# Three weight tiles of a GEMV moved from the input projection to W_out, and half of the last shift's weights moved to the end of the stream

## The chip, the cores and the metric

The kernel runs on one core of a Trainium2 chip. The metric is the device time of that core in microseconds (us): the median of three runs is given for a kernel, and one further execution was recorded by the profiler. Everything is in fp32.

## The reference

One residual block over a sequence of 256 tokens with 2048 features, conditioned by one vector `c` (adaLN). Cut to what matters:

```
mod = silu(c) @ w_ada + b_ada                      # 6 vectors of 2048
sh1, sc1, gt1, sh2, sc2, gt2 = split(mod, 6)
h = rms_norm(x, g_mix) * (1 + sc1) + sh1
qa, ka, va, qb, kb, vb = split(h @ w_in)           # 16 heads A (4 key heads), 16 heads B
o = concat[rms_norm(attention_A), rms_norm(attention_B)]
x = x + gt1 * (o @ w_out)
h = rms_norm(x, g_ffn) * (1 + sc2) + sh2
y = moe(h)      # top-1 group of 4, then top-2 of its 8 experts; 32 gated MLPs 2048-512-2048
x = x + gt2 * y
shf, scf = split(silu(c) @ w_ada_final + b_ada_final, 2)
out = rms_norm(x, g_final) * (1 + scf) + shf
```

The weights of the 32 experts are 403 MB of the 596 MB that are read. The products of a vector with `w_ada` and `w_ada_final` (GEMVs) need 117 MB more, and each weight of them is used once.

## The kernel before

**The stream.** All large weights pass through one ring of six slots of 2 MB in SBUF (class `Ring`, lines 42 to 79). Tiles are numbered in the order in which `ring.add` is called. SP loads tile i once the program has released tiles 0 to i−6 and the engine that used the slot is through with it (`pump`, issue at L70 and L72); a later tile never overtakes an earlier one. So the slowest consumer of an early tile holds up all loads behind it.

**Stages.** The first quarters (L294 to L360) form the first adaLN vectors, transpose and modulate x into `hT`, and compute the projections for the attention of kind A. Then a list `order` (L116 to L123) of 20 tiles for PE follows: 12 of `w_in` for the heads of kind B (`in_step`, L574) and 8 of `w_out` (`out_step`, L607). W_out tiles 0 to 3 multiply the A half of `o` and 4 to 7 the B half, each for 512 of the 2048 output columns and two token halves t, 8 products for each half; after each half DVE updates x from the PSUM bank `po` (L622). The B half is scaled by `r_oB`, which `norm_o` makes out of the sum of squares over all 16 heads (L539) by a matmul with ones (L546) and six small operations on DVE (L190 to L198).

**Vector tiles.** Behind each PE tile the table `VECTOR_TILES` (L39) puts so many vector tiles in the ring: 4 x 128 rows and 1024 columns of `w_ada` or `w_ada_final`. DVE sums them into an accumulator 128 x 1024, four operations for each (`vec_step`: L382 opens the accumulator, L384 adds). Four such tiles make one half of a vector. `vec_steps` takes them from a queue and stops where a new half begins while two accumulators are in use. An accumulator comes free with `vec_finish`, three turns after its last tile; that of a half of gt1 comes free when `spread_gt1(1)` or `spread_gt1(3)` has run, at W_out tiles 1 and 3. The halves stand in the order sh2, sc2, gt2, gt1, scf (two of each), then the first half of shf.

**Weaving.** In between PE's tiles `weave` advances the attention heads, which wait on the same DVE, and due items of the list `later`.

**Routing.** `router_turns(n)` and `router_products(n)` transpose x and form the router's logits. The second half of the shift vector shf (columns 1024 to 2047) is not summed by DVE: four ring tiles of 4 x 128 rows pass through PE with `cact` (silu of c, one column per 128 rows) broadcast as the stationary operand, 8 products for each tile, 32 in all (`shift_step`, L683 to L702). Then DVE finds group and experts, PE makes prefix sums (`pp`, L749 to L753), and the MoE begins: 8 passes over 4 experts each, gate and up products L829, down products L857.

**The end.** L1057 to L1078: the two rows of PSUM that make the last shift available on all partitions, the last norm, the scaled x plus shift, and the stores from ACT and SP.

Of the kernel before, what the change touches and what calls it, by code (L numbers as in the profile page):

```python
# [23 lines left out]
D = 2048  # L24
# [11 lines left out]
NEG = -1e30  # L36
RING = 6

VECTOR_TILES = [2, 3, 2, 3, 2, 3, 2, 3, 2, 3, 2, 3, 2, 2, 2, 2, 3, 2, 1, 0]  # L39


ROW_ADA, ROW_FIN, ROW_MIX, ROW_FFN, ROW_GFIN, ROW_OA, ROW_OB = 0, 24, 32, 36, 40, 44, 46
# [42 lines left out]
def block_kernel(ctx: ExitStack, tc: tile.TileContext, a: dict):  # L85
# [22 lines left out]
        first_quarters.append((gemv, [ring.add((2, 1536), rows(w_in, q * 512 + h * 256, 2, 0, 1536)) for h in range(2)]))  # L108

    vec_tiles = []  # L110
    for name, w, col in (("sh2", ada, 3 * D), ("sc2", ada, 4 * D), ("gt2", ada, 5 * D), ("gt1", ada, 2 * D), ("scf", fin, D), ("shf", fin, 0)):
        for c in (0,) if name == "shf" else (0, 1024):
            vec_tiles += [((name, c // 512), k, 4, 1024, rows(w, k * 512, 4, col + c, 1024)) for k in range(4)]
    blocks = [("qB0", 1536), ("kB0", 2560), ("vB0", 3584), ("qB1", 2048), ("kB1", 3072), ("vB1", 4096)]
    pe_tiles = [(name, h, rows(w_in, h * 1024, 8, col, 512)) for name, col in blocks for h in range(2)]
    pe_tiles += [("wo", h * 4 + n, rows(w_out, h * 1024, 8, n * 512, 512)) for h in range(2) for n in range(4)]  # L116
# [5 lines left out]
        order.append((name, h, part, extra))  # L122
    assert not vec_tiles  # L123

    shf_tiles = [ring.add((4, 1024), rows(fin, 512 * i, 4, 1024, 1024)) for i in range(4)]


    moe_tiles = []
    for g in range(8):
        e0 = 4 * g  # L130
        gu = []
        for J in range(4):
            for w in ("w_gate", "w_up"):
# [77 lines left out]
    with ExitStack() as sa:  # L211
# [305 lines left out]
        def values(kind, h):  # L517
# [12 lines left out]
            if h % 2:  # L530
# [3 lines left out]
                if c == 0:  # L534
                    S.activation(s, op[:, 0:256], AF.Square)
                else:
                    s2 = pa2.tile([128, SEQ], F32, tag="sq", name=f"sq{kind}{c}", bufs=1)
                    S.activation(s2, op[:, 0:256], AF.Square)
                    G.tensor_tensor(s, s, s2, op=ALU.add)  # L539
                if h == 15:  # L540
                    later.append([1, lambda: norm_o(kind)])

# [428 lines left out]
    for g in range(8):  # L971
# [56 lines left out]
        else:  # L1028
# [3 lines left out]
            for fc in range(4):  # L1032
# [33 lines left out]
    diag = pb1.tile([128, 128], F32, name="diag")
    S.activation(diag, ident, AF.Identity, scale=r3[:, 1:2])
    for J, y in last.items():
        c = slice(J * 512, (J + 1) * 512)
        PE.matmul(y, lhsT=diag, rhs=big[:, 1, c], start=False, stop=True)  # L1070
        S.copy(big[:, 1, c], y)  # L1071
        S.dma_start(out=out[:, 1, c], in_=big[:, 1, c])  # L1072
    for t, J, store in ((0, 0, 0), (0, 1, 2), (0, 2, 0), (0, 3, 2), (1, 0, 1)):
        c = slice(J * 512, (J + 1) * 512)
        V.scalar_tensor_tensor(big[:, t, c], big[:, t, c], r3[:, t : t + 1], shbc[:, c], op0=ALU.mult, op1=ALU.add)
        if store:
            c = slice((J + 1 - store) * 512, (J + 1) * 512)
            nc.sync.dma_start(out=out[:, t, c], in_=big[:, t, c])  # L1078
# [26 lines left out]
```

## Time and profile before

| | before |
|---|---|
| median of 3 runs | 1508.41 us (1505.83 to 1509.24) |
| the profiled execution | 1502.64 us, its span 1501.0 us |
| PE busy, share of the span | 1188.0 us, 79% |
| DVE busy | 499.0 us, 33% |
| HBM read | 596.02 MB, mean 398 GB/s over the span |
| granted TensorE clock, mean | 0.917 |

The span runs from the first to the last instruction. Times in the trace are counted from its start. The trace records each fp32 product of the program as two instructions: the 8 products of one half of a W_out tile read as x16. A granted clock of 1.00 is the upper of TensorE's two levels, 2.4 GHz.

### The profile page before, as it was taken

What the parts mean: (1) busy time and instruction counts of PE and PEld (TensorE: products, weight loads), DVE (VectorE), ACT (ScalarE), POOL (GpSimd) and SP (SyncE); (2) the same over time, 40 slices, a digit from 0 to 9 for tenths busy, and PEclk for the clock granted to TensorE, in tenths of its full rate; (3) what the DMA queues carried; (4) which work ended last, traced back from release to release, by engine and by line L of the source; (5) the groups of instructions that cost most, each with busy time, mean ns of one, the idle gap of its engine ahead of it and who ended that gap; (6) DMA issues with size and microseconds to landing.
All of it is one profiled execution on the core that took longest, in us unless ns stands there. A gap on an engine that the chain in (4) does not pass through costs nothing.

```text
span 1501.0 us, 14175 instructions
## 1 busy us (share of the span) xinstructions
PE 1188.0 (79%) x5891; PEld 525.8 (35%) x5892; DVE 499.0 (33%) x807; ACT 166.2 (11%) x423; POOL 157.5 (10%) x144
## 2 busy tenths in 40 slices
PE   4889999999999997777677767766767667667786
PEld 2667865754444542222212212211211211221222
DVE  1453789887667531011111211111201201111113
ACT  2000222223220110000000100000000000000012
POOL 1000355523441100000000000000000000000002
PEclk9999999999999999978978889889889988997999
DMA  9999999999987999999999999999999999999995
GB/s 333 396 392 399 394 402 402 402 401 400 355 317 302 388 380 422 421 420 421 421 421 421 421 421 422 422 422 421 421 420 422 422 422 422 421 421 421 421 412 210
DMA packets 125470, 599.38 MB, mean 399 GB/s; under 512 B 5881, under 2 KB 8489, under 8 KB 78041
## 3 DMA queue, kind: packets, MB, share of 16 engines
q1 hardware_dynamic: 121248, 594.82, 98.1%
q10 hardware_dynamic: 4120, 3.57, 0.7%
q8 instruction: 48, 0.79, 0.2%
q14 instruction: 22, 0.17, 0.0%
q0 software_dynamic: 32, 0.02, 0.0%
HBM read 596.02 MB, written 2.12 MB: 398 GB/s over the span
## 4 chain that ended last, share of the span: by engine, by line
DMA 45%; PE 11%; SPq 0%; issue 0%; ACT 0%; DVE 0%; ACTq 0%; DVEq 0%
DMA ring<-w_down 23%; DMA ring<-w_up 12%; DMA ring<-w_gate 10%; PE yp L857 5%; PE gp L829 2%; PE up L829 2%; PE sc_g L876 0%; SPq L70 0%; PE bc L770 0%; PE bc L771 0%; PE last L1060 0%; PE last L1059 0%; ACT big L1071 0%; PE last L1070 0%; ACTq L1072 0%
## 5 line engine op out<-in xcount | busy, mean ns | idle before, releaser
L857 PE MATMUL yp<-ring,actT_g 128*32 128x512 f32 x1024 | 181.5, 763 | 97.5 <-DMA ring<-w_down 91.7
L829 PE MATMUL up<-ring,xg_g 128*32 128x512 f32 x1024 | 177.3, 721 | 73.3 <-DMA ring<-w_up 73.2
L829 PE MATMUL gp<-ring,xg_g 128*32 128x512 f32 x1024 | 169.9, 703 | 69.3 <-DMA ring<-w_gate 68.8
L878 DVE TENSOR_TENSOR x<-x,sc_g 128x512 f32<-128x512 f32 x64 | 44.0, 688 | 252.3 <-PE sc_g L876 252.3
L618 PE MATMUL po<-ring,oT 128*128 128x512 f32 x256 | 118.0, 617 | 1.4 <-DMA ring<-w_out 1.4
L857 PEld LDWEIGHTS yp<-ring,actT_g 128*32 128x32 f32 x1024 | 39.3, 133 | 225.6 <-DMA ring<-w_down 130.9
L881 POOL TENSOR_TENSOR big<-x,xg_gscf 128x512 f32<-128x512 f32 x8 | 10.0, 1272 | 958.8 <-DVE x L878 958.8
L799 DVE TENSOR_SCALAR xg_g<-g_g,gsc,sh2c 128x128 f32<-128x128 f32 x64 | 26.2, 410 | 249.8 <-PE g_g L790 232.5
L829 PEld LDWEIGHTS up<-ring,xg_g 128*32 128x32 f32 x1024 | 38.4, 127 | 197.5 <-DMA ring<-w_up 105.9
L829 PEld LDWEIGHTS gp<-ring,xg_g 128*32 128x32 f32 x1024 | 38.0, 123 | 186.5 <-DMA ring<-w_gate 99.5
L797 ACT ACTIVATE xg_g<-g_g,sh2c,gsc 128x128 f32<-128x128 f32 x64 | 29.3, 458 | 503.9 <-DVE xg_g L799 503.9
L384 DVE SCALAR_TENSOR_TENSOR acc_gt<-ring,cact,acc_gt 128x1024 f32<-128x1024 f32 x60 | 79.2, 1321 | 1.6
L870 DVE TENSOR_TENSOR ys_g<-yp,gt2bc 128x512 f32<-128x512 f32 x32 | 21.8, 690 | 171.8 <-PE yp L857 171.8
L618 PEld LDWEIGHTS po<-ring,oT 128*128 128x128 f32 x256 | 49.7, 198 | 63.6 <-issue 61.1
L790 PEld LDWEIGHTS g_g<-pn_g,big 128*128 128x128 f32 x512 | 60.5, 194 | 29.1 <-issue 28.2
L790 PE MATMUL g_g<-pn_g,big 128*128 128x128 f32 x512 | 66.7, 284 | 1.4 <-DVE pn_g L782 1.4
L348 PE MATMUL qA<-hT,ring 128*128 128x256 f32 x256 | 61.6, 396 | 4.8 <-DVE hT L343 3.5
L876 PE MATMUL sc_g<-ys_g,smat_g 128*128 128x512 f32 x128 | 63.4, 618 | 1.6 <-DVE ys_g L870 1.6
L585 PE MATMUL pw_vB<-ring,hT 128*128 128x512 f32 x128 | 56.7, 597 | 2.9 <-DMA ring<-w_in 2.9
L589 PE MATMUL pw_kB<-hT,ring 128*128 128x256 f32 x256 | 57.0, 381 | 1.2 <-DMA ring<-w_in 1.2
L589 PE MATMUL pw_qB<-hT,ring 128*128 128x256 f32 x256 | 56.5, 381 | 0.2 <-DMA ring<-w_in 0.2
L348 PEld LDWEIGHTS qA<-hT,ring 128*128 128x128 f32 x256 | 50.7, 199 | 13.1 <-DVE hT L343 4.3
(329 smaller groups left out, 1125.4 us busy)
## 6 DMA issues: line engine op xcount, KB each, us to landing
ring<-w_gate SPq DMA_DIRECT2D x64, 2048.0 KB, 20.3
ring<-w_up SPq DMA_DIRECT2D x64, 2048.0 KB
ring<-w_down SPq DMA_DIRECT2D x62, 2048.0 KB, 20.4
ring<-w_ada SPq DMA_DIRECT2D x32, 2048.0 KB, 17.0
ring<-w_ada SPq DMA_DIRECT2D x32, 1024.0 KB, 14.1
ring<-w_ada_final SPq DMA_DIRECT2D x16, 2048.0 KB, 11.0
ring<-w_in SPq DMA_DIRECT2D x12, 2048.0 KB, 16.8
ring<-w_out SPq DMA_DIRECT2D x8, 2048.0 KB
```

The source lines that it names most:

```text
L348: PE.matmul(early[n // 2][:, (n % 2) * 256 : (n % 2 + 1) * 256], lhsT=w[:, n * 128 : (n + 1) * 128], rhs=hT[:, kk, :], start=kk == 0 and n ...
L384: V.scalar_tensor_tensor(accs[name], w[:, kk, :], cact[:, c : c + 1], accs[name], op0=ALU.mult, op1=ALU.add)
L585: PE.matmul(b[s], lhsT=hT[:, kk, s * 128 : (s + 1) * 128], rhs=w[:, k, :], start=kk == 0, stop=kk == 15)
L589: PE.matmul(b[s][:, n * 256 : (n + 1) * 256], lhsT=w[:, k, c * 128 : (c + 1) * 128], rhs=hT[:, kk, :], start=kk == 0 and n == 0, stop=kk = ...
L618: PE.matmul(b, lhsT=oT[:, (i // 4) * 8 + k, t * 128 : (t + 1) * 128], rhs=w[:, k, :], start=k == 0, stop=k == 7)
L790: PE.matmul(pm[:, i * 128 : (i + 1) * 128], lhsT=big[:, t, kk * 128 : (kk + 1) * 128], rhs=pn[:, t, :], start=t == 0 and i == 0, stop=t == ...
L797: S.activation(xg[:, kk, :], pm[:, i * 128 : (i + 1) * 128], AF.Identity, bias=sh2c[:, kk : kk + 1], scale=gsc2[:, kk : kk + 1])
L799: V.tensor_scalar(xg[:, kk, :], pm[:, i * 128 : (i + 1) * 128], gsc2[:, kk : kk + 1], sh2c[:, kk : kk + 1], op0=ALU.mult, op1=ALU.add)
L829: PE.matmul(bankt[32 * e : 32 * e + 32, :], lhsT=xg[:, kk, 32 * e : 32 * e + 32], rhs=w[e // 2][:, e % 2, j, :], start=kk == 0, stop=kk == ...
L857: PE.matmul(y[32 * e : 32 * e + 32, :], lhsT=aT[:, fc, 32 * e : 32 * e + 32], rhs=w(e)[:, n * 512 : (n + 1) * 512], start=fc == 0, stop=fc ...
L876: PE.matmul(pm, lhsT=sm[:, t * 128 : (t + 1) * 128], rhs=ys[:, n, :], start=True, stop=True)
L878: V.tensor_tensor(x1[:, t, c], x1[:, t, c], pm, op=ALU.add)
```

## The change

Three things are changed. (1) `VECTOR_TILES` gives 27 instead of 30 vector tiles to the input projection and 17 instead of 14 to W_out, and the halves of the vectors are queued in another order: both halves of gt1 ahead of the second half of gt2. (2) The second half of shf is split into two blocks of 512 columns. The first (columns 1024 to 1535) is loaded as two tiles of 8 x 128 rows during routing, 16 products, all behind the router's last products. The second (1536 to 2047) comes as two such tiles behind the last tile of the MoE, and the last sums, copies and updates are written anew for it. (3) The sum of squares of the last head is added on DVE instead of POOL.

```
-VECTOR_TILES = [2, 3, 2, 3, 2, 3, 2, 3, 2, 3, 2, 3, 2, 2, 2, 2, 3, 2, 1, 0]
+VECTOR_TILES = [2, 2, 3, 2, 2, 2, 3, 2, 2, 3, 2, 2, 3, 2, 3, 3, 3, 2, 1, 0]
...
+    for i in (0, 1, 2, 3, 4, 6, 7, 5, 8, 9, 10):
+        name, w, col, c = halves[i]
+        vec_tiles += [((name, c // 512), k, 4, 1024, rows(w, k * 512, 4, col + c, 1024)) for k in range(4)]
...
-    shf_tiles = [ring.add((4, 1024), rows(fin, 512 * i, 4, 1024, 1024)) for i in range(4)]
+    shf_tiles = [ring.add((8, 512), rows(fin, 1024 * i, 8, 1024, 512)) for i in range(2)]
...
+    last_block = [(c0, c1, ring.add((c1 - c0, 512), rows(fin, c0 * 128, c1 - c0, 1536, 512))) for c0, c1 in ((0, 8), (8, 16))]
...
-                    G.tensor_tensor(s, s, s2, op=ALU.add)
+                    (V if h == 15 else G).tensor_tensor(s, s, s2, op=ALU.add)
...
-            for k in range(4):
-                for J in (2, 3):
-                    PE.matmul(
-                        shift[32 * J : 32 * J + 32, :], lhsT=cact[:, 4 * i + k : 4 * i + k + 1].to_broadcast([128, 32]),
-                        rhs=w[:, k, (J - 2) * 512 : (J - 1) * 512], start=i + k == 0, stop=i + k == 6, skip_group_check=True,
-                    )
+            for k in range(8):
+                q = 64 + 32 * (k % 2)
+                PE.matmul(
+                    shift[q : q + 32, :], lhsT=cact[:, 8 * i + k : 8 * i + k + 1].to_broadcast([128, 32]),
+                    rhs=w[:, k, :], start=i == 0 and k < 2, stop=i == 1 and k > 5, skip_group_check=True,
+                )
...
-        shift_step(0)
         router_turns(3)
-        shift_step(1)
         router_products(3)
-        for i in (2, 3):
+        for i in range(2):
             shift_step(i)
...
-                    spread(R["shf"], ROW_FIN, shbc)
+                    spread(R["shf"], ROW_FIN, shbc, range(2))
+                    four = pb1.tile([128, 2], F32, name="four")
+                    V.tensor_reduce(four[:, 0:1], ident[:, 0:128:32], axis=AX.X, op=ALU.add)
+                    V.tensor_reduce(four[:, 1:2], ident[:, 64:128:32], axis=AX.X, op=ALU.add)
+                    pm = mbank("m", "bc", 2)
+                    PE.matmul(pm, lhsT=four[:, 1:2].to_broadcast([128, 128]), rhs=R["shf"], start=True, stop=False)
+                    PE.matmul(pm, lhsT=pick(ROW_FIN + 2, 128), rhs=pr, start=False, stop=True)
+                    S.copy(shbc[:, 1024:1536], pm)
...
-    last = {1: mbank("g", "last1", 1), 2: mbank("u", "last2", 1), 3: mbank("y", "last3", 4)}
...
+    last = {1: mbank("g", "last1", 1), 2: mbank("u", "last2", 1)}
+    tail = mbank("y", "tail", 4)
+    part = mbank("y", "part", 4)
...
+    for c0, c1, idx in last_block:
+        w = ring.get(idx)
+        for c in range(c0, c1):
+            q = 32 * (c % 4)
+            PE.matmul(
+                part[q : q + 32, :], lhsT=cact[:, c : c + 1].to_broadcast([128, 32]), rhs=w[:, c - c0, :],
+                start=c < 4, stop=c > 11, skip_group_check=True,
+            )
+        ring.release(idx)
+
+    sums = pb.tile([128, 2, 512], F32, tag="ys", name="sums")[:, 0, :]
+    S.copy(sums, part)
...
+    PE.matmul(tail, lhsT=four[:, 0:1].to_broadcast([128, 128]), rhs=sums, start=False, stop=True)
...
-        S.dma_start(out=out[:, 1, c], in_=big[:, 1, c])
-    for t, J, store in ((0, 0, 0), (0, 1, 2), (0, 2, 0), (0, 3, 2), (1, 0, 1)):
+    S.dma_start(out=out[:, 1, 512:1536], in_=big[:, 1, 512:1536])
+    for t, J, store in ((0, 0, 0), (0, 1, 2), (0, 2, 0), (0, 3, 2), (1, 3, 1), (1, 0, 1)):
         c = slice(J * 512, (J + 1) * 512)
-        V.scalar_tensor_tensor(big[:, t, c], big[:, t, c], r3[:, t : t + 1], shbc[:, c], op0=ALU.mult, op1=ALU.add)
+        V.scalar_tensor_tensor(big[:, t, c], big[:, t, c], r3[:, t : t + 1], tail if J == 3 else shbc[:, c], op0=ALU.mult, op1=ALU.add)
```

In W_out the lines of the changed kernel are numbered four higher (L384 there is L388, L622 is L626).

DVE in the second W_out tile, before; `hT<-po` is an update after one token half, `ISA` with `spB` and `biasB` a head's scores, `denB` the reciprocal of its sums, `acc_...` the vector tiles' operations:

```order
L503 RECIPROCAL denB_2107<-denB_2107 128x2
L382 TENSOR_SCALAR acc_scf_2113<-ring_1925,cact 128x1024
L384 SCALAR_TENSOR_TENSOR acc_scf_2113<-ring_1925,cact,acc_scf_2113 128x1024 x3
L622 SCALAR_TENSOR_TENSOR hT<-po_2118,r_oA,hT 128x512
L384 SCALAR_TENSOR_TENSOR acc_scf_2113<-ring_1943,cact,acc_scf_2113 128x1024 x2
L485 ISA stB_2156,mxB_2157<-spB_2148,biasB_2041 128x128
```

The same place in the changed order (the first row lies between the two updates of W_out tile 1):

```order
L388 SCALAR_TENSOR_TENSOR acc_gt_2070<-ring_1824,cact,acc_gt_2070 128x1024 x2
L388 SCALAR_TENSOR_TENSOR acc_gt_2070<-ring_1859,cact,acc_gt_2070 128x1024 x2
L507 RECIPROCAL denB_2085<-denB_2085 128x2
L388 SCALAR_TENSOR_TENSOR acc_gt_2070<-ring_1859,cact,acc_gt_2070 128x1024 x2
L388 SCALAR_TENSOR_TENSOR acc_gt_2070<-ring_1908,cact,acc_gt_2070 128x1024 x4
L626 SCALAR_TENSOR_TENSOR hT<-po_2101,r_oA,hT 128x512
L388 SCALAR_TENSOR_TENSOR acc_gt_2070<-ring_1985,cact,acc_gt_2070 128x1024 x2
L489 ISA stB_2139,mxB_2140<-spB_2131,biasB_2016 128x128
L489 ISA mxB_2140 128x1
```

The accumulations of three tiles (rings 1824, 1859 and 1908) now stand almost without a break ahead of that update, where before one tile's four stood.

DVE from the first update of W_out tile 3 to the norm of the B half (`rv_oB` to `r_oB`), before:

```order
L622 SCALAR_TENSOR_TENSOR hT<-po_2287,r_oA,hT 128x512
L382 TENSOR_SCALAR acc_scf_2307<-ring_2129,cact 128x1024
L384 SCALAR_TENSOR_TENSOR acc_scf_2307<-ring_2129,cact,acc_scf_2307 128x1024 x3
L622 SCALAR_TENSOR_TENSOR hT<-po_2312,r_oA,hT 128x512
L384 SCALAR_TENSOR_TENSOR acc_scf_2307<-ring_2168,cact,acc_scf_2307 128x1024 x4
L190 TENSOR_SCALAR rv_oB<-pnB 128x2
L194 RECIPROCAL r_oB<-rl_oB 128x2
L195 TENSOR_TENSOR rl_oB<-r_oB 128x2
L196 TENSOR_TENSOR rl_oB<-rl_oB,rv_oB 128x2
L197 TENSOR_SCALAR rl_oB<-rl_oB 128x2
L198 TENSOR_TENSOR r_oB<-r_oB,rl_oB 128x2
L622 SCALAR_TENSOR_TENSOR hT<-po_2356,r_oB,hT 128x512
```

The same place now, up to the first operation of the norm:

```order
L626 SCALAR_TENSOR_TENSOR hT<-po_2258,r_oA,hT 128x512
L386 TENSOR_SCALAR acc_scf_2282<-ring_2083,cact 128x1024
L388 SCALAR_TENSOR_TENSOR acc_scf_2282<-ring_2083,cact,acc_scf_2282 128x1024 x3
L626 SCALAR_TENSOR_TENSOR hT<-po_2289,r_oA,hT 128x512
L543 TENSOR_TENSOR sqB<-sqB,sqB_2303 128x256
L388 SCALAR_TENSOR_TENSOR acc_scf_2282<-ring_2095,cact,acc_scf_2282 128x1024 x4
L388 SCALAR_TENSOR_TENSOR acc_scf_2282<-ring_2110,cact,acc_scf_2282 128x1024 x4
L388 SCALAR_TENSOR_TENSOR acc_scf_2282<-ring_2151,cact,acc_scf_2282 128x1024 x4
L386 TENSOR_SCALAR acc_scf_2326<-ring_2221,cact 128x1024
L388 SCALAR_TENSOR_TENSOR acc_scf_2326<-ring_2221,cact,acc_scf_2326 128x1024 x3
L388 SCALAR_TENSOR_TENSOR acc_scf_2326<-ring_2287,cact,acc_scf_2326 128x1024 x4
L194 TENSOR_SCALAR rv_oB<-pnB 128x2
```

One tile of four operations stood between the second update and the norm; five tiles of four stand there now, and the square sum (L543) ahead of them.

SP's loads around W_out tiles 4 and 5, before. Rings are numbered in stream order, and the waits name the engine whose release the load needs (PE or DVE) beside the loads that it follows:

```order
L72 DMA ring77_2168<-w_ada_final 128x4x1024 [waits DMAHW7_49,DMAHW6_49,DVE_49]
L72 DMA ring78_2242<-w_out 128x8x512 [waits DMAHW0_49,PE_49]
L72 DMA ring79_2244<-w_ada_final 128x4x1024 [waits DMAHW2_49,DVE_49]
L72 DMA ring80_2275<-w_ada_final 128x4x1024 [waits DMAHW3_49,DMAHW1_49,DVE_49]
L72 DMA ring81_2321<-w_ada_final 128x4x1024 [waits DMAHW5_49,DVE_49]
L72 DMA ring82_2323<-w_out 128x8x512 [waits DMAHW4_49,PE_49]
L72 DMA ring83_2337<-w_ada_final 128x4x1024 [waits DMAHW6_49,DVE_49]
```

The same now:

```order
L72 DMA ring77_2287<-w_ada_final 128x4x1024 [waits DMAHW0_49,DVE_49]
L72 DMA ring78_2310<-w_out 128x8x512 [waits DMAHW7_49,DMAHW3_49,PE_49]
L72 DMA ring79_2316<-w_ada_final 128x4x1024 [waits DMAHW1_49,DVE_49]
L72 DMA ring80_2318<-w_ada_final 128x4x1024 [waits DMAHW2_49,DVE_49]
L72 DMA ring81_2324<-w_ada_final 128x4x1024 [waits DMAHW4_49,DVE_49]
L72 DMA ring82_2331<-w_out 128x8x512 [waits DMAHW5_49,DVE_49]
L72 DMA ring83_2337<-w_ada_final 128x4x1024 [waits DMAHW6_49,DVE_49]
```

The load of W_out tile 5 (`ring82`) waited for PE and now waits for DVE (its tile b1). Tile 4 (`ring78`) still waits for PE, behind the load of b2 (`ring77`), which waits for DVE.

## Rows read from the trace of the kernel before

**Rows 1.** Page, 40 equal slices of the span: GB/s moved.

```profile
GB/s 333 396 392 399 394 402 402 402 401 400 355 317 302 388 380 422 421 420 421 421 421 421 421 421 422 422 422 421 421 420 422 422 422 422 421 421 421 421 412 210
```

**Rows 2.** Stretches: busy us (x count) per engine, granted clock, DMA share, GB/s.

```profile
300.00:361.00 61.00, 57.16 (x235) 32.22 (x234) 47.75 (x84) 18.78 (x54) 15.65 (x19) 1.00 1.03 401
439.00:470.00 31.00, 27.89 (x68) 12.36 (x67) 20.99 (x23) 4.02 (x8) 7.71 (x4) 0.89 0.74 283
560.00:1460.00 900.00, 643.55 (x3562) 197.75 (x3558) 132.85 (x207) 47.32 (x96) 0.00 (x0) 0.88 1.01 421
```

**Rows 3.** SP timeline: start us, us, what; the seventh MoE tile's issue.

```profile
547.18 1.11 SPq L72 DMA_DIRECT2D ring<-w_up  x2
```

**Rows 4.** PE's waits, 190 to 361.5 us: total us, times, longest.

```profile
PE pw_vB L585 <- DMA ring<-w_in: 2.9, 1, 2.9
PE po L618 <- DMA ring<-w_out: 1.4, 1, 1.4
PE pw_kB L589 <- DMA ring<-w_in: 1.2, 1, 1.2
```

**Rows 5.** DVE groups by line, 340 to 520 us: busy us, mean ns, idle.

```profile
L384 DVE SCALAR_TENSOR_TENSOR acc_scf<-ring,cact,acc_scf 128x1024 f32<-128x1024 f32 x30 | 43.9, 1465 | 0.8
L384 DVE SCALAR_TENSOR_TENSOR acc_gt<-ring,cact,acc_gt 128x1024 f32<-128x1024 f32 x22 | 29.2, 1327 | 0.5
...
L382 DVE TENSOR_SCALAR acc_scf<-ring,cact 128x1024 f32<-128x1024 f32 x2 | 1.5, 738 | 0.0
```

**Rows 6.** PE timeline in W_out: start us, us, what, [idle before <-releaser].

```profile
451.54 0.95 PE L546 MATMUL pnB<-ones,sqB 128*128 128x1 f32 x4 [3.12 <-POOL sqB L539]
452.35 23.88 PE L618 MATMUL po<-ring,oT 128*128 128x512 f32 x48
...
485.79 7.11 PE L618 MATMUL po<-ring,oT 128*128 128x512 f32 x16
```

**Rows 7.** DVE timeline in W_out.

```profile
440.09 4.82 DVE L384 SCALAR_TENSOR_TENSOR acc_scf<-ring,cact,acc_scf 128x1024 f32<-128x1024 f32 x3
446.76 0.75 DVE L622 SCALAR_TENSOR_TENSOR hT<-po,r_oA,hT 128x512 f32<-128x512 f32 x1 [1.85 <-PE po L618]
447.42 6.46 DVE L384 SCALAR_TENSOR_TENSOR acc_scf<-ring,cact,acc_scf 128x1024 f32<-128x1024 f32 x4
...
455.02 0.16 DVE L198 TENSOR_TENSOR r_oB<-r_oB,rl_oB 128x2 f32<-128x2 f32 x1
```

**Rows 8.** DMA issues: KB each, us to landing; a load with none ahead.

```profile
x<-x SPq DMA_DIRECT2D x1, 2048.0 KB, 8.6
```

**Rows 9.** PE timeline in routing and at the first MoE products.

```profile
530.21 7.06 PE L691 MATMUL shift<-ring,cact 128*32 128x512 f32 x32
537.20 0.41 PE L749 MATMUL pp<-oT,tri 128*128 128x32 f32 x2
...
543.27 3.88 PE L829 MATMUL gp<-ring,xg_g 128*32 128x512 f32 x32 [0.51 <-DVE xg_g L799]
```

**Rows 10.** DVE timeline in routing: the last operation ahead of the prefix products.

```profile
534.82 0.22 DVE L746 TENSOR_TENSOR oT<-gh,h 128x64 f32<-128x64 f32 x1
```

**Rows 11.** Chain that ended last, 1440 to 1501 us: start us, us, what.

```profile
1467.32 16.21 DMA ring<-w_down
```

**Rows 12.** PE timeline at the end.

```profile
1470.98 1.92 PE L857 MATMUL yp<-ring,actT_g 128*32 128x512 f32 x16 [1.75 <-DMA ring<-w_down]
...
1478.40 1.06 PE L857 MATMUL yp<-ring,actT_g 128*32 128x512 f32 x8 [0.68 <-DMA ring<-w_down]
...
1487.27 1.02 PE L1059 MATMUL last<-R_shf,ident 128*128 128x512 f32 x2
```

**Rows 13.** ACT timeline at the end: last copy and last store issue.

```profile
1495.54 0.59 ACT L1071 COPY big<-last 128x512 f32<-128x512 f32 x1 [0.43 <-PE last L1070]
1496.15 0.34 ACTq L1072 DMA_DIRECT2D out<-big  x1
```

**Rows 14.** DVE timeline at the end.

```profile
1491.31 3.40 DVE L1075 SCALAR_TENSOR_TENSOR big<-big,r_n,xg_shbc 128x512 f32<-128x512 f32 x5
```

More of the change, by code (lines that the diff above doesn't have):

```diff
@@ L110, in block_kernel @@
     vec_tiles = []
-    for name, w, col in (("sh2", ada, 3 * D), ("sc2", ada, 4 * D), ("gt2", ada, 5 * D), ("gt1", ada, 2 * D), ("scf", fin, D), ("shf", fin, 0)):
-        for c in (0,) if name == "shf" else (0, 1024):
-            vec_tiles += [((name, c // 512), k, 4, 1024, rows(w, k * 512, 4, col + c, 1024)) for k in range(4)]
+    halves = [(n, w, col, c) for n, w, col in (("sh2", ada, 3 * D), ("sc2", ada, 4 * D), ("gt2", ada, 5 * D), ("gt1", ada, 2 * D), ("scf", fin, D), ("shf", fin, 0)) for c in (0, 1024)]
+    for i in (0, 1, 2, 3, 4, 6, 7, 5, 8, 9, 10):
+        name, w, col, c = halves[i]
+        vec_tiles += [((name, c // 512), k, 4, 1024, rows(w, k * 512, 4, col + c, 1024)) for k in range(4)]
     blocks = [("qB0", 1536), ("kB0", 2560), ("vB0", 3584), ("qB1", 2048), ("kB1", 3072), ("vB1", 4096)]
@@ L1054, in block_kernel @@
             further_rounds()
-    last = {1: mbank("g", "last1", 1), 2: mbank("u", "last2", 1), 3: mbank("y", "last3", 4)}
-    for J, y in last.items():
-        PE.matmul(y, lhsT=pick(32 * J, 128), rhs=R["shf"], start=True, stop=False)
-        PE.matmul(y, lhsT=pick(ROW_FIN + J, 128), rhs=pr, start=False, stop=False)
     sst3 = pb1.tile([128, 2], F32, name="sst3")
@@ L1064, in block_kernel @@
     out = a["out"].rearrange("(t p) n -> p t n", p=128)
+    last = {1: mbank("g", "last1", 1), 2: mbank("u", "last2", 1)}
+    tail = mbank("y", "tail", 4)
+    part = mbank("y", "part", 4)
+    PE.matmul(tail, lhsT=pick(ROW_FIN + 3, 128), rhs=pr, start=True, stop=False)
+    PE.matmul(last[1], lhsT=pick(32, 128), rhs=R["shf"], start=True, stop=False)
+    PE.matmul(last[2], lhsT=four[:, 1:2].to_broadcast([128, 128]), rhs=R["shf"], start=True, stop=False)
+    for J, y in last.items():
+        PE.matmul(y, lhsT=pick(ROW_FIN + J, 128), rhs=pr, start=False, stop=False)
+    for c0, c1, idx in last_block:
[9 more added lines that the diff above has]
+    S.copy(sums, part)
     diag = pb1.tile([128, 128], F32, name="diag")
     S.activation(diag, ident, AF.Identity, scale=r3[:, 1:2])
+    PE.matmul(tail, lhsT=four[:, 0:1].to_broadcast([128, 128]), rhs=sums, start=False, stop=True)
     for J, y in last.items():
```

## The prediction

> **What bounds the kernel now.** I read the page's slices first. The row of transferred bytes stays near 400 GB/s up to the tenth slice, falls to 355, 317 and 302 in slices 11 to 13, and stands at 421 from about slice 16 to the end [rows 1]. So there are three regimes, and the table by stretches gives each of them its numbers [rows 2]. From 300 to 361 us, the input projection, the DMA share is 1.03. From 439 to 470 us, inside W_out, it is 0.74 at 283 GB/s, while PE is busy 27.89 of 31 us. In the MoE, 560 to 1460 us, it is 1.01 while PE is busy 644 of 900 us. The MoE is a stream: it ends a fixed time after it starts. Its start is read from SP's timeline: six MoE tiles fit the ring, and the seventh is issued at 547.18 [rows 3], right after the first 32 gate products that began at 543.27 [rows 9]. What makes those products earlier or later moves the whole rest by the same amount. So the places to watch are the waits of PE up to 361 us, PE and DVE in W_out, PE in routing, and what comes after the last landing.
>
> **Up to the first W_out tile: three vector tiles fewer.** PE waits there for weights three times: 2.9, 1.4 and 1.2 us, together 5.5 [rows 4]. Each vector tile that no longer stands in the queue brings the next tiles forward by its passage (2.1 MB at 401 GB/s [rows 2], 5.2 us), so I let all three waits go: −5.5. What is late next is DVE: in the second W_out tile the new order gives it 12 accumulations, 10 of them ahead of an update and all of them ahead of two heads' scores. At 1.33 us each [rows 5] 12 are 16 us, against 14.2 us of PE work for one W_out tile (one of its halves, x16 in the trace, takes 7.11 [rows 6]; I count products as the trace does, two for each of the program). I take +3 for it, near the one wait of this kind that the trace shows, 3.12 us [rows 6]. It can be 0, or a full half of the products, 7. Net −2.5, between −5.5 and +1.5.
>
> **W_out.** Here the order matters more than the count. Only two accumulators may be open. The one of gt1's second half closes with W_out tile 3, and beside it gt2's second half, now queued behind gt1, is still being summed in tile 2. So the scf tiles, although loaded earlier, are not consumed until tile 3's first update. In before, DVE had one vector tile of 4 operations between that W_out tile's second update (446.76) and the six small operations of the norm, which end at 455.2 [rows 7]. Now it has five: 20 operations. I count in before's times and call these tiles a2, a3, a4, b1 and b2; a1 is the one ahead of them.
>
> DVE first. Tile a1 is done at 440.09 + 4.82 = 444.9 [rows 7]; the second update ends at 447.5, and the square sum that moves to DVE at about 448.5. From there I count 1.465 us each, the mean of 30 scf accumulations, and 0.74 for the first operation of b1, which opens an accumulator [rows 5]: a2 ends at 454.4, a3 at 460.2, a4 at 466.1, b1 at 471.2, b2 at 477.1. The norm takes 1.4 more, 478.5.
>
> Then the loads. Slots come free in that order, and the W_out tiles queue behind them on SP. The load of b2 waits for a1, 444.9. It is then alone in the queue, and a lone 2 MB load took 8.6 us [rows 8]: 453.5. W_out tile 4 comes 5.2 us behind it: 458.7, where its products started at 452.35 [rows 6]. Tile 5 was loaded when PE released tile 3; now it waits for b1 on DVE, 471.2, and lands 8.6 later, at 479.8 (the three loads ahead of it are down by 474.7). In before its first 16 products started at about 476.2 − 7.1 = 469.1, at the end of the 23.88 us row [rows 6]. So tile 5 is +10.7.
>
> The clock comes on top. After the 3.12 us wait of before, 48 products took 23.88 us where three times 7.11 is 21.3 [rows 6], and the granted clock of 439 to 470 is 0.89, below the upper level of 2.4 GHz for a part of it [rows 2]. I charge these 2.6 us once more for the second wait. Together +13.3. From tile 6 on I see no further wait: its slot comes free with b3, and tile 5's products and the transposes among them last 16.7 us (469.1 to 485.79 [rows 6]).
>
> From below: 1.327 us for each accumulation [rows 5], 5.2 us instead of 8.6 for the load, and no slower clock give b1 at 469.1 and a landing at 474.3: +5.2. From above: four accumulations took 6.46 us at this very place [rows 7], 1.61 each; then b1 ends at 473.5 and tile 5 lands at 482.1, +13.0, and with the clock's price at both waits +18.2.
>
> A rule bears on the clock's share. The rows differ: after the 3.12 us wait the clock was low, but the stretch 300 to 361, with the 2.9 us wait in it, was granted 1.00 [rows 2, 4]. The Trainium skill, "TensorE: Matmul & The Clock Gate", section "Loop structure matters more than you think", says that a loop that waits for a DMA ahead of every output tile leaves the matmuls cold. Going by that rule the sum below stays at +9.2; going by the row of 300 to 361 it would be +6.6.
>
> The square sum of the last head goes from POOL to DVE. POOL's is what ended the 3.12 us wait, but the weights of tile 4 now land later than that anyway, so I give it nothing.
>
> **Routing.** Of 64 shift products 32 go; the last 32 took 7.06 us [rows 9]. A part of that was cover: the router's last products wait for hT, which DVE and ACT make out of the last transposes, and 16 shift products stood in between. I count 1.6 as cover: −5.5. If nothing was cover it is −7.1; if one block of 16 was, −3.5. DVE's own chain ends at 535.04 [rows 10], two us before PE's prefix products at 537.20 [rows 9], and with all 32 products behind the router's PE still ends last. Two tiles less to load ahead of the MoE give nothing more, since its start hangs on routing and not on bytes.
>
> **The end.** Before, the last weights landed at 1467.32 + 16.21 = 1483.53 [rows 11], 17.5 us ahead of the span's end. Now two tiles follow. The last landings lie 1483.53 − 1478.40 = 5.13 us apart [rows 11, 12]: 10.3. Behind the last: 16 products 1.92, one 512-column product (x2) 1.02 [rows 12], a copy 0.59 [rows 13], three updates at 3.40/5, 2.0 [rows 14], an issue of 0.34 and the 4.5 us from the last issue's end to the span's end [rows 13], and 0.7 for hand-overs: 11.1. That is 21.4 in place of 17.5: +3.9. The norm, after which the updates began at 1491.31 [rows 14], 7.8 after the old last landing, becomes hidden. Bounds: +3.2 without hand-overs; +9 if tiles with 2 KB rows pass half as fast again. Those in routing then cost nothing visible, since the stream has room there. The sums of identity columns and the third shift block are four small instructions beside the MoE stream, whose DVE is busy 133 of 900 us [rows 2]: 0, and 0.5 if they fell on the path.
>
> **Sum.** −2.5 + 13.3 − 5.5 + 3.9 = +9.2 on the profiled execution's 1502.6, so 1511.8. The median of the runs is 1508.4, 5.8 above that execution: 1518.
>
> **Rivals.**
> 1. Everything fits. DVE works off its pile at 1.327 us, the loads behind it pass in 5.2 us, all three early waits go with nothing in their place, and all of the 7.1 us in routing: −5.5 + 5.2 − 7.1 + 3.9 = −3.5, so 1505. For it: in 300 to 361 DVE was busy 47.75 of 61 us with the clock at 1.00 [rows 2], so a busy DVE need not hurt. Against it: the scf accumulations took 1.465 in the mean. The change wins where W_out costs less than the 4.1 that my other three terms bring, or the 8.7 that they bring here. Chance 0.17.
> 2. The pile costs more: the upper bound in W_out (+18.2), and DVE late in the second tile (+1.5 net): 1.5 + 18.2 − 5.5 + 3.9 = +18.1, so 1526. For it: 6.46 us for four accumulations beside POOL's work. Against it: POOL has one sum less there. Chance 0.20.
> 3. It cancels: W_out at its lower bound, the rest as I take it, −2.5 + 5.2 − 5.5 + 3.9 = +1.1, so 1509. Chance 0.15.
> That the three tiles do not do what moving them says (the early waits stay, because the tile before is what is late) would put 5.5 on top of my sum, 1523; it shares rival 2's chance.
>
> **Chances and range.** The forecast has 0.48. A measurement of this kernel can tell about 0.2%, 3 us. Faster holds rival 1 and a little of rival 3: 0.18. Within it: 0.15. Slower: the forecast and rival 2, 0.67. The range goes from rival 1 to a little past rival 2, 1505 to 1528. The forecast's own range is 1512 to 1523.
>
> **What would show it.** In the changed profile: the waits for w_in gone; DVE with 20 accumulations between tile 3's second update and the norm; a wait of PE for w_out ahead of tile 4 and another of some 5 us ahead of tile 5, with a granted clock below 1 behind them; the prefix products some 5 us sooner after W_out's last product; the span's end about 21 us after the last landing. No wait of PE for w_out there, or a first gate product before 543 us, would make the forecast wrong.

## The result, and the profile after

| | median, us | runs | ratio to before, 95% interval |
|---|---|---|---|
| before | 1508.83 (1505.83 to 1509.60) | 4 | |
| changed | 1524.24 (1517.81 to 1529.62) | 4 | 1.0104 [1.0062, 1.0146] |

The change costs about 15.5 us. Its profiled execution took 1517.81 us, span 1516.2, which is 15.2 over that of before; the one is the lowest of the four runs of the changed kernel, the other lies under the four of before. So the two traces can be set against each other, term by term.

The slices first (answer to [rows 1]): the trough now has 299 and 230 in the eleventh and twelfth slice and another 303 in the fifteenth.

```profile
GB/s 336 396 392 400 390 402 395 373 400 347 299 230 394 396 303 422 421 420 421 421 421 421 421 421 421 421 421 422 421 421 421 421 421 422 421 421 421 421 409 265
```

The stretches (columns as in [rows 2]): the projection and the MoE are as they were. In 439 to 470 PE is busy 20.85 of 31 us instead of 27.89, at a granted clock of 0.83 in the mean, and from 470 to 500 DVE is busy 28.86 of 30.

```profile
300.00:361.00 61.00, 59.75 (x245) 34.71 (x244) 48.23 (x87) 19.40 (x57) 15.28 (x17) 1.00 1.03 401
439.00:470.00 31.00, 20.85 (x56) 9.20 (x55) 25.69 (x22) 3.09 (x5) 2.97 (x2) 0.83 0.75 282
470.00:500.00 30.00, 25.17 (x61) 10.83 (x59) 28.86 (x32) 2.77 (x9) 4.80 (x3) 0.89 1.02 394
560.00:1460.00 900.00, 643.19 (x3600) 197.54 (x3592) 134.27 (x212) 46.45 (x95) 0.00 (x0) 0.88 1.01 421
```

PE's timeline (answers to [rows 6]) gives the landmarks. The first product of W_out starts at 358.75, against 361.44 in before. The second half of tile 3 ends at 449.1, against 446.6: what was ahead is now behind. Tile 4 waits 8.32 us for its weights and tile 5 another 3.48, and its first 16 products take 9.96 us.

```profile
358.75 7.03 PE L622 MATMUL po<-ring,oT 128*128 128x512 f32 x16
...
442.11 7.03 PE L622 MATMUL po<-ring,oT 128*128 128x512 f32 x16
...
451.77 0.58 PE L550 MATMUL pnB<-ones,sqB 128*128 128x1 f32 x4 [1.83 <-DVE sqB L543]
460.66 15.53 PE L622 MATMUL po<-ring,oT 128*128 128x512 f32 x32 [8.32 <-DMA ring<-w_out]
...
481.91 9.96 PE L622 MATMUL po<-ring,oT 128*128 128x512 f32 x16 [3.48 <-DMA ring<-w_out]
```

PE's waits behind 361 us (engine, line, releaser: us in total, times, longest). The two for w_out, ahead of tiles 4 and 5, are new; those of the heads' transposes for POOL's softmax sum to 5.8 us, where before had 2.5 in two such rows (1.7 and 0.8).

```profile
PE po L622 <- DMA ring<-w_out: 11.8, 2, 8.3
PE tpB L516 <- POOL stB L509: 3.5, 6, 0.8
PE tpB L516 <- POOL stB L508: 2.3, 3, 1.1
```

DVE's timeline (answers to [rows 7]): 12 accumulations without a break at 451.55, the opened accumulator, 7 more at 468.05, and the norm ends at 478.55, where it ended at 455.2.

```profile
441.60 4.82 DVE L388 SCALAR_TENSOR_TENSOR acc_scf<-ring,cact,acc_scf 128x1024 f32<-128x1024 f32 x3
...
451.55 15.80 DVE L388 SCALAR_TENSOR_TENSOR acc_scf<-ring,cact,acc_scf 128x1024 f32<-128x1024 f32 x12
...
468.05 9.21 DVE L388 SCALAR_TENSOR_TENSOR acc_scf<-ring,cact,acc_scf 128x1024 f32<-128x1024 f32 x7
...
478.39 0.16 DVE L202 TENSOR_TENSOR r_oB<-r_oB,rl_oB 128x2 f32<-128x2 f32 x1
...
480.08 5.95 DVE L388 SCALAR_TENSOR_TENSOR acc_scf<-ring,cact,acc_scf 128x1024 f32<-128x1024 f32 x4
```

SP's timeline (answers to [rows 3]): tile 4's load goes out at 449.17 behind that of b2, tile 5's at 472.00, when b1's last accumulation is done, and the seventh MoE tile at 556.82, 9.6 us later than before.

```profile
449.17 0.37 SPq L72 DMA_DIRECT2D ring<-w_out  x1
...
472.00 0.37 SPq L72 DMA_DIRECT2D ring<-w_out  x1
...
556.82 0.88 SPq L72 DMA_DIRECT2D ring<-w_up  x2
```

Routing, PE and DVE (answers to [rows 9, 10]): 32 shift products, the prefix products two us behind DVE's last mask, the first gate products at 553.16 in place of 543.27.

```profile
540.41 7.06 PE L696 MATMUL shift<-ring,cact 128*32 128x512 f32 x32
547.40 0.41 PE L752 MATMUL pp<-oT,tri 128*128 128x32 f32 x2
...
553.16 3.64 PE L832 MATMUL gp<-ring,xg_g 128*32 128x512 f32 x32 [1.34 <-DVE xg_g L802]
```

```profile
545.07 0.23 DVE L749 TENSOR_TENSOR oT<-gh,h 128x64 f32<-128x64 f32 x1
```

The chain at the end (answer to [rows 11]): the last landing at 1504.30, then products, copy, product, and 11.9 us to the span's end.

```profile
1484.50 19.80 DMA ring<-w_ada_final
...
1504.34 1.97 PE part L1083 x16
...
1506.33 0.59 ACT sums L1090
...
1506.97 1.12 PE tail L1093 x2
...
1509.85 0.59 ACT big L1097
```

### The profile page after: what moved, and what is told of

It reads as the page before. It is cut to its first block, busy times and chain, and to the rows that moved or that the text cites. A ratio compares the mean times of both kernels' runs of the same rounds, so it can differ in the third digit from the quotient of the medians.

```text
span 1516.2 us, 14167 instructions
## 1 busy us (share of the span) xinstructions
PE 1184.4 (78%) x5885; PEld 522.7 (34%) x5886; DVE 497.8 (33%) x812; ACT 166.0 (11%) x422; POOL 149.2 (10%) x142
## 4 chain that ended last, share of the span: by engine, by line
DMA 46%; PE 10%; issue 0%; SPq 0%; ACT 0%; DVE 0%; DVEq 0%
DMA ring<-w_up 22%; DMA ring<-w_gate 12%; DMA ring<-w_down 11%; PE up L832 4%; PE yp L860 2%; PE gp L832 2%; DMA ring<-w_ada_final 1%; PE sc_g L879 0%; PE part L1083 0%; PE last L1096 0%; SPq L72 0%; PE tail L1093 0%; PE sm_g L823 0%; ACT sums L1090 0%; ACT big L1097 0%
## 5 line engine op out<-in xcount | busy, mean ns | idle before, releaser
L622 PE MATMUL po<-ring,oT 128*128 128x512 f32 x256 | 119.3, 622 | 11.8 <-DMA ring<-w_out 11.8
L388 DVE SCALAR_TENSOR_TENSOR acc_gt<-ring,cact,acc_gt 128x1024 f32<-128x1024 f32 x60 | 79.4, 1323 | 1.6
L622 PEld LDWEIGHTS po<-ring,oT 128*128 128x128 f32 x256 | 50.3, 200 | 74.6 <-issue 61.9
```

The source lines that it names most:

```text
L388: V.scalar_tensor_tensor(accs[name], w[:, kk, :], cact[:, c : c + 1], accs[name], op0=ALU.mult, op1=ALU.add)
L622: PE.matmul(b, lhsT=oT[:, (i // 4) * 8 + k, t * 128 : (t + 1) * 128], rhs=w[:, k, :], start=k == 0, stop=k == 7)
```

## The experiments

All were timed in five rounds beside the kernel before. The last column is (ratio − 1) times the median of before on the same chip.

| run | median, us | before | ratio, 95% interval | us to before |
|---|---|---|---|---|
| e1 old table, old order | 1501.50 | 1503.86 | 0.9982 [0.9968, 0.9997] | −2.7 |
| e2 new table, old order | 1511.64 | 1503.86 | 1.0044 [1.0031, 1.0057] | +6.6 |
| e3 old table, new order | 1521.48 | 1503.86 | 1.0111 [1.0096, 1.0125] | +16.7 |
| e4 before, square sum on DVE | 1500.16 | 1503.86 | 0.9971 [0.9958, 0.9985] | −4.4 |
| e5 early spread | 1509.81 | 1504.83 | 1.0036 [1.0017, 1.0056] | +5.4 |
| e6 no last block | 1495.59 | 1504.83 | 0.9929 [0.9905, 0.9953] | −10.7 |
| e7 permuted projection | 1500.12 | 1504.83 | 0.9964 [0.9947, 0.9982] | −5.4 |
| e8 new table, early spread, old end | 1512.78 | 1504.83 | 1.0040 [1.0023, 1.0057] | +6.0 |
| e9 one tile moved | 1500.91 | 1505.84 | 0.9965 [0.9951, 0.9980] | −5.3 |
| e10 one tile back | 1507.27 | 1505.84 | 1.0004 [0.9986, 1.0022] | +0.6 |
| e11 end in 4 KB rows | 1503.17 | 1505.84 | 0.9981 [0.9963, 0.9999] | −2.9 |
| e12 two tiles moved | 1501.86 | 1505.25 | 0.9974 [0.9959, 0.9989] | −3.9 |

**Table against order (e1 to e3).** The theory: the loss is a pile on DVE that the order of the halves makes. The rival: three tiles more beside W_out are too many.

```
e1 = changed, with
-VECTOR_TILES = [2, 2, 3, 2, 2, 2, 3, 2, 2, 3, 2, 2, 3, 2, 3, 3, 3, 2, 1, 0]
+VECTOR_TILES = [2, 3, 2, 3, 2, 3, 2, 3, 2, 3, 2, 3, 2, 2, 2, 2, 3, 2, 1, 0]
-    for i in (0, 1, 2, 3, 4, 6, 7, 5, 8, 9, 10):
+    for i in (0, 1, 2, 3, 4, 5, 6, 7, 8, 9, 10):
e2 = changed, with the second of these edits; e3 = changed, with the first
```

> The changed kernel with the table and the order of the vector halves of before; routing, end and square sum stay changed. Pile theory (the loss is made of the scf operations queued on DVE ahead of the norm): PE waits for neither W_out tile 4 nor tile 5, the +2.5 us at the end of W_out tile 3 and the +13.5 behind it go, and what is left is routing (-5.9) and the end (+5.6): 1505 to 1509 us, the lower figure if the square sum on DVE is worth 3 us. Rival (the end and the routing carry the loss): 1517 or more.

> The changed kernel with the table of before (30 and 14) and the new order of the halves (gt1 ahead of gt2's second half). The program order keeps 20 operations ahead of the norm. If the order of the halves makes the pile: waits of PE for tile 4 (about 8 us) and tile 5 (3 us or more) stay, 1519 to 1528 us. If the count does: 1505 to 1510.

> The changed kernel with the order of the halves of before (gt2 whole ahead of gt1) and its own table (27 and 17). The program order then has 8 operations between W_out tile 3's second update and the norm instead of 20. If the order of the halves makes the pile: no wait for tiles 4 and 5, 1502 to 1508 us, up to 3 us under the kernel with the old table as well, since one wait for w_in of 2.9 us is gone too. If the three tiles more beside W_out are what DVE or the loads cannot take: 1518 or more, with waits for w_out left.

e3 keeps the loss with the count of before, and e1, which differs from it in the order alone, is 20 us faster and has no wait for w_out behind 361 us. In e3 the waits for w_out are there, 19.7 us in four pieces, 8.0 of them ahead of tile 4 and 3.9 ahead of tile 5:

```profile
PE po L622 <- DMA ring<-w_out: 19.7, 4, 8.0
```

Two windows show where the work went (columns as in [rows 2]); first e1, then e3. In e3 DVE does 15.6 us less from 357 to 455, because the scf halves may not be opened; from 455 to 515 it is busy 58.18 of 60 us, and PE 48.69 instead of 60.00.

```profile
357.00:455.00 98.00, 91.35 (x285) 42.03 (x284) 61.21 (x104) 23.45 (x73) 40.02 (x37) 0.93 0.87 331
455.00:515.00 60.00, 60.00 (x185) 30.01 (x185) 50.03 (x54) 8.87 (x23) 10.79 (x7) 1.00 0.98 378
```

```profile
357.00:455.00 98.00, 83.88 (x262) 38.15 (x260) 45.65 (x92) 21.98 (x68) 33.55 (x36) 0.98 0.68 257
455.00:515.00 60.00, 48.69 (x129) 22.47 (x130) 58.18 (x57) 4.52 (x13) 7.59 (x5) 0.89 1.03 388
```

e2 missed its 1502 to 1508. No wait for w_out is left in it, as expected, but PE waits for DVE at the spreads of gt1, ahead of W_out tiles 0 and 2:

```profile
359.81 2.02 PE L431 MATMUL pm_bc<-acc_gt,ones 128*128 128x512 f32 x2 [4.42 <-DVE denB L507]
...
414.97 2.08 PE L431 MATMUL pm_bc<-acc_gt,ones 128*128 128x512 f32 x2 [4.47 <-DVE acc_gt L388]
```

With 27 tiles in the projection and gt1 last, gt1's sums are late; its first half is spread at 359.81 before its last tile is added (four accumulations at 374.96), so the gate of e2 lacks a part of the sum. Against e1, which differs in the table alone, e2 is 9.3 us slower (uncertain by some 3), and these two waits are 8.9. The new order is what makes the new table possible, and the new order makes the pile.

**The accumulators (e5).**

```
-            if i < 4:
-                spread_gt1(i)
+            for J in {0: (0,), 1: (1, 2, 3)}.get(i, ()):
+                spread_gt1(J)
```

> The changed kernel with its table and its order of halves, but the spreads of gt1 for tiles 1, 2 and 3 all run at the start of W_out tile 1, so that the accumulator of gt1's second half closes two tiles earlier. Loads, products and sums are the same. The program order then has 8 operations between tile 3's second update and the norm. If the closed accumulators make the loss: PE's waits for W_out tiles 4 and 5 go, and the time falls by about 13 us, to between 1 us under and 4 us over the kernel before. If three vector tiles more beside W_out are too many wherever they are summed: 10 us or more over before, with waits for w_out.

The pile is gone with both edits of the change still in, and so are the waits for w_out: the time falls from +15.7 (1.0104) to +5.4. It is not the −1 to +4 that was expected. Against e1, which has neither edit, e5 is still 8.1 us slower (uncertain by some 4). So the rival holds a part: the three tiles cost something of their own, without waits for w_out. What is left are waits of the heads, 10.1 us, and 2.4 at the spreads now put behind each other:

```profile
PE tpB L516 <- POOL stB L508: 5.9, 3, 4.4
PE tpB L516 <- POOL stB L509: 4.2, 6, 1.3
PE pm_bc L431 <- ACT hT L433: 2.4, 2, 1.7
```

**The square sum alone (e4).**

```
 before, with
-                    G.tensor_tensor(s, s, s2, op=ALU.add)
+                    (V if h == 15 else G).tensor_tensor(s, s, s2, op=ALU.add)
```

> The kernel before with one edit alone: the last head's sum of squares on DVE. The 3.12 us wait of the norm's matmul on POOL becomes about 1 us. If the slow 48 products behind it (23.88 us for 21.3) come from that wait, they run at 7.1 each 16 as well: -2 to -5 us, 1504 to 1507. If the wait has other causes behind it (DVE's four accumulations are then ahead of nothing new): no difference, 1508 to 1510.

The wait is 0.86 us instead of 3.12, and the 48 products behind it take 20.85 us where they took 23.88 [rows 6]. Six other traces with a wait of 0.86 or 1.30 us there (e1, e6, e7, e9, e10 and e12) have 20.85 too. This edit is worth 4.4 us by itself (uncertain by 2); in the changed kernel an 8 us wait covers it.

```profile
451.04 0.58 PE L546 MATMUL pnB<-ones,sqB 128*128 128x1 f32 x4 [0.86 <-DVE sqB L539]
451.48 20.85 PE L618 MATMUL po<-ring,oT 128*128 128x512 f32 x48
```

**The end (e6, e11).**

```
e6 = e1, with
-    last_block = [(c0, c1, ring.add(...)) for c0, c1 in ((0, 8), (8, 16))]
+    last_block = []
-    S.copy(sums, part)
+    V.memset(sums, 0.0)
e11 = e1, with
-    last_block = [(c0, c1, ring.add((c1 - c0, 512), rows(fin, c0 * 128, c1 - c0, 1536, 512))) ...
+    last_block = [(c0, c1, ring.add(((c1 - c0) // 2, 1024), rows(fin, c0 * 128, (c1 - c0) // 2, 1024, 1024))) ...
```

> e1 (table and order of before) without the two last tiles: the shift of columns 1536 to 2047 is neither loaded nor multiplied (zeros stand in its place, so those columns of the output lack it). What this gains over e1 is the price of the two tiles at the end. By the forecast's term: 3.9 us, that is about 6 us under before. By the spans behind the first gate product (957.7 and 958.6 without the two tiles, 963.0 to 965.8 with them): 5.5 to 8, that is 8 to 10 us under before.

> e1 with the two last tiles read in 4 KB rows (4 blocks of 128 rows and 1024 columns each, the same bytes and products; the shift of the last 512 columns is then made of other weights). In e1 the two tiles took from 1472.7 to 1489.2, 16.4 us, where four w_down tiles of 1 MB ahead of them passed in about 12 together. If rows of 2 KB are the reason: the landing comes 2 us or more sooner, 4 to 5 us under before. If the drain of the queue behind the last load is: no difference from e1, 2 to 3 under before.

e6 is 8.0 us under e1, uncertain by some 4, and the spans of the two traces behind the first gate product, 965.8 and 957.8, differ by the same 8.0: the two tiles cost about twice the forecast's 3.9. Rows of 4 KB make no difference that shows: e11 is level with e1. PE's timeline of e1 at the end shows what the price is made of besides the loads:

```profile
1479.66 1.06 PE L860 MATMUL yp<-ring,actT_g 128*32 128x512 f32 x8 [2.54 <-DMA ring<-w_down]
1481.54 3.39 PE L879 MATMUL sc_g<-ys_g,smat_g 128*128 128x512 f32 x4 [0.81 <-DVE ys_g L873]
1484.76 1.02 PE L1074 MATMUL tail<-pr,ident 128*128 128x512 f32 x2
...
1489.15 3.64 PE L1083 MATMUL part<-ring,cact 128*32 128x512 f32 x32
1493.49 1.12 PE L1093 MATMUL tail<-sums,four 128*128 128x512 f32 x2 [0.70 <-ACT sums L1090]
```

The last down products wait for their weights until 1479.66. From there PE runs on almost without a gap: the last sums, five 512-column products that prepare the shift (from 1484.76, 4.4 us), and all 32 of the last block. PE waits for neither tile of that block, so PE, not the last landing, sets the end, though by little: the DMA share falls to 0.00 at 1489.60, and the second tile's products begin at about 1490.9. Putting the five ahead of the last down products was not tried; going by these times it could save some 1.3 us, an estimate. And the last w_down comes later: 942.9 us behind the first gate product (at 536.81), against 940.3 in before.

**How many tiles, and where (e7 to e10, e12).** All start from e4. e7 and e10 move tiles within or into the projection, e9 and e12 move one and two tiles to W_out with the order of before, e8 takes the table, the order and e5's spreads.

```
e7  VECTOR_TILES = [2, 2, 3, 2, 3, 2, 3, 3, 2, 3, 2, 3, 2, 2, 2, 2, 3, 2, 1, 0]
e9  VECTOR_TILES = [2, 2, 3, 2, 3, 2, 3, 2, 3, 2, 3, 2, 3, 2, 2, 2, 3, 2, 1, 0]
e10 VECTOR_TILES = [2, 3, 2, 3, 3, 3, 2, 3, 2, 3, 2, 3, 2, 2, 2, 1, 3, 2, 1, 0]
e12 VECTOR_TILES = [2, 2, 3, 2, 3, 2, 3, 2, 2, 3, 2, 2, 3, 2, 3, 2, 3, 2, 1, 0]
```

> The kernel before with the square sum on DVE (e4) and the same 30 vector tiles beside the input projection in another order: 2, 2, 3, 2, 3, 2, 3, 3, 2, 3, 2, 3. One tile fewer is then ahead of pw_vB0's weights. If the wait of 2.6 us there is set by the tiles ahead of it, it goes, and the time is 4 to 7 us under before. If the time lost is only moved to the next wait: as e4, 3 to 4 us under before.

> The table, the order of halves and the square sum of the changed kernel with the early spreads of e5, but routing and the end of before (four shift tiles ahead of the MoE, none behind). If the table is worth the waits that it takes out of the projection once no pile follows: e4's gain and 2 to 3 us more, 5 to 7 us under before. If the early part is worth nothing: as e4, 3 to 4 under.

> e4 (before with the square sum on DVE) with one vector tile moved from the projection to W_out tile 0 (29 and 15) and the order of halves of before. If every tile more beside W_out costs its four accumulations on a DVE that the heads wait for: 1 to 4 us over e4, that is 0 to 3 under before. If one tile fits and a wait for w_in goes: 5 to 7 us under before.

> e4 with one vector tile moved the other way, from W_out tile 3 to the third PE tile of the projection (31 and 13). If DVE is what W_out waits for: W_out gains some of the tile's 5.3 us of DVE time, and the projection, whose DMA share is 1.03 already, loses up to the 5.2 us of its passage: between 2 us under and 3 over e4, 2 to 6 under before. If the stream alone counts: 5 us over e4, 1 over before.

> e4 with two vector tiles moved to W_out (28 and 16), order of halves, routing and end of before. One tile moved measured 5.3 us under before, three with the spreads pulled forward 6.0 us over. If DVE's time beside W_out has a limit that the second tile is still under: 4 to 7 us under before. If each tile behind the first costs its four accumulations (5.3 us): about level with before, 1 under to 2 over.

One or two tiles moved (−5.3, −3.9) and a projection in another order (−5.4) are all level with e4 (−4.4): their intervals overlap. So two tiles fit beside W_out, but they gain nothing that shows. The traces show that the waits for weights went in one of the three only: in e4 PE waits 2.6 us for `pw_vB`; in e7 it waits 2.8 for `pw_kB` instead, in e9 still 2.0 for `pw_vB`, and in e12, without a wait for w_in, 4.4 us for DVE at the first spread of gt1. The times of e7 and e9 lie where the wait was expected to be gone, without its being gone. One tile more in the projection costs about 5 us (e10 against e4, uncertain by some 3). The passage of a 2 MB tile there is 5.2, but since one tile fewer (e9) gives nothing back, that this is the cause is not shown. e8 missed: the third tile with its order costs 10 us over e4 even with the early spreads. In its trace the heads wait as in e5. Whether DVE's time or only the place of the spreads sets that, these runs don't tell apart.

No complete version tried beats e4, e7, e9 and e12 by more than the intervals; all four are faster than both kernels. e4, one changed line, is the simplest of them.

## Why the prediction came out as it did

The forecast was 1518 and the measured median is 1524.24: inside the whole range of 1505 to 1528, but 1 us above the forecast's own 1512 to 1523.

**The mechanism held.** W_out is +13.5 us between the two profiled executions (from the end of tile 3 to the end of tile 7: 446.6 to 518.4 before, 449.1 to 534.4 after), forecast +13.3. The steps agree with the trace, shifted by the 2.5 us that tile 3 ends later: tile 4 at 458.7 + 2.5 = 461.2 against 460.66, tile 5 at 479.8 + 2.5 = 482.3 against 481.91. e3 and e5 show the cause: the order alone brings the pile, and closing an accumulator earlier takes it away. That the size came out so near is in part luck, as the next paragraph shows.

**A price inside it was off, and another balanced it.** I took 1.465 us for an scf accumulation. The 12 took 15.80, 1.317 each, and tile 5's load, which waits for b1, went out at 472.00, 1.7 earlier than 471.2 + 2.5. From there the load took 9.9 us, not 8.6, with three loads ahead of it. Of the clock I charged 2.6 us for the second wait: tile 5's first half took 9.96, 2.85 more than 7.11. The 32 products behind the first wait took 15.53, 1.3 more than 2 x 7.11.

**The clock.** Behind the two waits for w_out the granted clock was 0.50, the lower level: from 460.66 to 462.50 behind the wait of 8.32 us, during which it had fallen already (0.59 in the mean of 452.00 to 460.60), and from 481.91 to 486.00 behind the wait of 3.48 us. The longer wait cost its products less, 1.3 us against 2.85. The sum that kept the clock's price was the nearer one. The Trainium skill, "TensorE: Matmul & The Clock Gate", section "Loop structure matters more than you think", tells of a loop with a long DMA wait ahead of each tile that its matmuls run cold; for these two single waits the trace agrees (columns as in [rows 2]).

```profile
452.00:460.60 8.60, 0.34 (x4) 0.26 (x3) 8.39 (x7) 0.02 (x1) 0.00 (x0) 0.59 1.04 388
481.91:484.00 2.09, 2.09 (x3) 1.06 (x4) 2.06 (x2) 0.00 (x0) 0.39 (x1) 0.50 1.02 408
```

But e4's 0.86 us wait left the 48 products at full speed, and two kernels with the same 1.84 us wait at this place differ: behind it 16 products took 8.81 us in e5 and 7.11 in e8 (first e5, then e8). The length of the one wait ahead does not decide it.

```profile
456.94 0.58 PE L550 MATMUL pnB<-ones,sqB 128*128 128x1 f32 x4 [1.84 <-DVE sqB L543]
457.38 8.81 PE L622 MATMUL po<-ring,oT 128*128 128x512 f32 x16
```

```profile
460.89 0.58 PE L547 MATMUL pnB<-ones,sqB 128*128 128x1 f32 x4 [1.84 <-DVE sqB L540]
461.33 7.11 PE L619 MATMUL po<-ring,oT 128*128 128x512 f32 x16
```

**The projection stays open.** Forecast −2.5, between −5.5 and +1.5; this pair of traces shows +2.5 at the end of tile 3. The early waits did go (2.7 us ahead at the first W_out product), but the heads' transposes wait longer, by 3.3 us, a sum of gt2 (`pm_gt`) moved behind the start of W_out, 1.0, and the rest is spread over small waits. One pair of traces does not settle such a term: e4, e1 and e6, which are the kernel before up to the square sum, ended tile 3 at 448.4, 452.0 and 452.2, 1.8 to 5.5 us later than before, so that against e1 the changed kernel's 449.1 is 2.9 ahead. e9 and e12, with one and two tiles moved, are within 1 us of e4, uncertain by some 3. For three tiles no run separates this term from W_out.

**Routing** is −5.85 from W_out's last product to the prefix products (18.8 to 13.0), forecast −5.5, and 0.3 less from there to the first gate product. All of this reached the MoE's start, as forecast. e6, which has the routing and the square sum of the change but not its table, its order or its two last tiles, agrees: −6.2 and e4's −4.4 make −10.6, and it measured −10.7.

**The end was mis-sized.** From the first gate product to the span's end it is 957.7 before and 963.0 after, +5.3, and +8.0 by e6 against e1, uncertain by some 4. The term was 3.9. In the changed kernel the last landing is 11.1 us further back (1504.30 − 1483.53 − 9.64 of the stream's later start) in place of 10.3, and 11.9 us lie behind it in place of 11.1. In e1 it is PE's queue of products, which the term left out: I counted what stands behind the last landing and not what stands ahead of the last block's products on PE. The 21 us that the prediction set behind the last landing are counted from the last w_down; from the last landing itself its terms give the 11.1. The norm was hidden, as said.

**The sum:** +2.5 + 13.5 − 6.2 + 5.3 = +15.1 against +9.2, with 5.0 of the difference in the projection, as this pair of traces has it, and 1.4 at the end. Rival 1 (all fits) fell with the 8.3 us wait; rival 2, +18.1, was nearer in size than the forecast but not for its reason, as its DVE price of 1.61 did not come; rival 3 fell with W_out. The edit that I gave nothing, the square sum, gave nothing that shows in this kernel and 4.4 us by itself.

## What to carry to other kernels

A tile's load has two ends: where it stands in the queue, and when its consumer is allowed to take it. In a ring that frees its slots in order, a consumer that is barred (here by two accumulators) holds back loads of another engine, so after any change of an order count the operations between the last free point and the next one that others wait for. What a wait saves is a gain only if the stage behind it has no wait of its own; and a load moved behind the last one pays its passage and what its consumer still has to do, ahead of its products and behind them.

## What the runs showed of the hardware

- A DVE accumulation of 128 x 1024 took 1.317 us in the mean of 12 with POOL idle, and about 1.49 when POOL copied beside it (four in 5.95 us at 480.08, above, 2.08 of them beside the copy). POOL's timeline of the changed kernel has its gap just there. The Trainium skill, "SBUF — State Buffer", section "Who interferes with whom", says that a DVE instruction with two SBUF inputs contends with a GpSimd instruction that reads SBUF; these rows agree.

```profile
450.08 1.27 POOL L627 TENSOR_TENSOR x<-x,hT 128x512 f32<-128x512 f32 x1 [7.38 <-DVE hT L626]
480.22 2.08 POOL L629 COPY big<-x 128x512 f32<-128x512 f32 x1 [28.88 <-DVE x L627]
```

- When no load follows, the DMA share falls step by step over several microseconds, so the end of a stream is slower than its passage. In the changed kernel, while the last tile lands (columns as in [rows 2]), it is 1.04, 0.73, 0.41 and 0.22. The Trainium skill, "DMA: Bandwidth & Descriptors", section "Why a DMA increments its semaphore by 16 and not by 1", says that a DMA runs on up to 16 engines that finish independently, and that it counts as landed with the last; a falling mean share is what that would look like, but no row here shows the engines one by one.

```profile
1489.00:1494.00 5.00, 4.10 (x28) 1.05 (x24) 2.07 (x3) 1.80 (x5) 3.52 (x3) 1.00 1.04 376
...
1497.00:1500.00 3.00, 3.00 (x8) 1.33 (x7) 1.94 (x4) 1.45 (x4) 2.29 (x2) 1.00 0.73 276
1500.00:1502.00 2.00, 2.00 (x9) 0.65 (x11) 1.47 (x7) 0.20 (x1) 0.21 (x1) 1.00 0.41 152
1502.00:1504.00 2.00, 1.85 (x16) 0.34 (x16) 1.66 (x3) 0.00 (x0) 0.00 (x0) 1.00 0.22 84
```
